# Squares of a recurrence taken on pairs, eight instead of four buffers for split weights, a later start of attention and a last output tile in halves, in one hybrid attention and recurrence layer

## The chip, the core and the metric

The kernel runs on one core of one Trainium2 chip, in one launch, in float32. The metric is the device time in microseconds (us) of a launch. The names of the engines are those of the profile: PE is the matrix engine, DVE the vector engine, ACT the scalar engine, POOL the general engine, SP the engine that issues most transfers.

## The reference

One layer on 512 tokens of width 2048. A normalized input is projected by `w_in` to queries, keys, values, two gates and the input of a gated linear recurrence. Eight heads of attention and a recurrence in both directions are each normalized, gated, and projected together by `w_out`.

```python
h = rms_norm(x, norm_w)
proj = h @ w_in                                  # (512, 2048) @ (2048, 4608)
q, k, v, g_attn, xr, g_lru = split(proj, SPLITS)
attn_out = attention_group(q, k, v, ...)         # RMS norm and rotation of q, k; softmax(q k) v; 8 heads
lru_out = lru_group(xr, ...)                     # h_fwd + h_bwd of two first-order recurrences over the tokens
mixed = concatenate([rms_norm(attn_out, attn_norm_w) * silu(g_attn),
                     rms_norm(lru_out, lru_norm_w) * silu(g_lru)])
return x + mixed @ w_out
```

Inside the recurrence: `a = exp(-8 r softplus(-lam))`, `h[t] = a[t] h[t-1] + sqrt(1 - a[t]^2) (i[t] xf[t])`, where `r` and `i` are sigmoids of two block-diagonal products.

## The kernel before

Every product is made of three matmuls: each operand is split into a high part (a rounding of the number, by a cast on ACT) and a low part (the rest, by a subtraction on DVE), and high x high, high x low and low x high are added up in PSUM (`mm3`, L142). For the weights this is `wsplit` (L195 to L201): a transfer brings 256 rows x 512 columns (`wr`, three buffers), and for each of the two halves of 128 rows (`k` is 0 or 1) ACT casts `wh` (L199) and DVE subtracts `wl` (L200). Tags `wh` and `wl` have four buffers each in the pool `xw`, two chunks' worth. A projection to 512 columns is eight such chunks; each chunk is four steps of six matmuls, and each step needs both halves of the chunk (`proj_feat`, `tok_block`).

The program runs in this order: the input is transposed, then the recurrence's input is projected (tag `pj`, PSUM banks), then the first half of the recurrence (`lru_half(0)`) beside the second half's projection, then the projection of keys and values (`kv_proj`) beside `lru_half(1)`, then the two projections of queries (`both`, that is `q_proj` twice) beside `kv`, which normalizes and rotates keys, then attention beside three gate projections (`gates`), then the last gate projection and the output projection (`outputs`). `weave` puts a stated number of projection steps between the pieces of a chain: where a chain yields 8, eight steps of six matmuls come next. The order of PE's instructions is therefore written out by hand. The order on ACT, DVE and POOL is made by a scheduler from priorities; each engine then works strictly in that order, and a wait holds everything behind it.

The recurrence goes by pairs of 128 channels (`lru_pair`, L374): products on PE, sigmoids on ACT (L407), then tanh (L417), exponentials (L423) and square roots (L427) on ACT, then on DVE L430, L431, four scans (L434) and two additions (L440) that write the pair's sum `hs`. L442 and L444 take the squares of `hs` on ACT, and L445 adds them up on POOL, for the norm.

Pools lie on two sides of SBUF, `left` and `right`. A pool opened where another was closed gets its memory, and each new tile there waits for the last use of the old tiles that lay in it (`reuse_waits="tile"`). After `kv_proj` the pool `lru`, with the recurrence's tiles `b4` and `k2`, is closed and `qkv` and `rot` are opened on the same side. `evac_tok` (L470, ACT) empties the PSUM banks of keys and values, so that the query projection can use them.

Of the kernel before, what the change touches and what calls it, by code (L numbers as in the profile page):

```python
# [55 lines left out]
def hybrid_kernel(  # L56
# [49 lines left out]
    def nm(s):  # L106
        cnt[0] += 1
        return f"{s}_{cnt[0]}"
# [77 lines left out]
    def wraw(w, r0, c0, nk=1):  # L186
# [3 lines left out]
        for k in range(nk):  # L190
            ks = slice(k * 2 // nk, (k + 1) * 2 // nk)
            nc.sync.dma_start(raw[:, ks, :], src[:, ks, :])
            yield raw

    def wsplit(raw, k):  # L195
# [3 lines left out]
        nc.scalar.copy(hi, raw[:, k, :])  # L199
        nc.vector.tensor_sub(lo, raw[:, k, :], f(hi))  # L200
        return hi, lo  # L201
# [172 lines left out]
    def lru_pair(n0, xrs, grs, steps, rest):  # L374

        xcs, cs, rs, is_, ths = [], [], [], [], []
        for n, xr, gr in zip((n0, n0 + 1), xrs, grs):
            with tc.high_priority(AHEAD // 2):
                gh, gl = k2(F32R, (P, 4, P)), k2(F32R, (P, 4, P))
                nc.scalar.copy(gh, gr)  # L380
                nc.vector.tensor_sub(gl, gr, f(gh))

                xc = k2()
                xcs.append(xc)
                nc.scalar.activation(
                    xc, xr, AF.Identity, bias=v1(R_CB + n), scale=v1(R_CW + 2 * NB + n)
                )
                for j, o in ((0, -2), (1, -1), (3, 1)):
                    d0, d1 = max(0, -o), SEQ - max(0, o)
                    nc.vector.scalar_tensor_tensor(  # L390
                        xc[:, d0:d1], xr[:, d0 + o : d1 + o], v1(R_CW + j * NB + n),
                        xc[:, d0:d1], op0=ALU.mult, op1=ALU.add,
                    )
                ch, cl = k2(F32R), k2(F32R)
                nc.scalar.copy(ch, xc)
                nc.vector.tensor_sub(cl, xc, f(ch))
                cs.append((gh, gl, ch, cl))
        for b, n in enumerate((n0, n0 + 1)):
            yield steps[b]
            gh, gl, ch, cl = cs[b]  # L400
            rs.append(b4())
            is_.append(b4())
            for dst, j0, bias in ((rs[b], 0, R_BA), (is_[b], 2, R_BX)):
                for d in range(2):
                    pg = mm()
                    mm3(pg, gh[:, j0 + d, :], gl[:, j0 + d, :], ch, cl, True, True)
                    nc.scalar.activation(  # L407
                        dst[:, d, :], pg, AF.Sigmoid, bias=v1(bias + d * NB + n)
                    )
            i = is_[b]  # L410
            nc.vector.tensor_mul(i, i, xcs[b][:, None, :].broadcast_to([P, 2, SEQ]))
        yield rest
        for b, n in enumerate((n0, n0 + 1)):
            ths.append(b4())
            for d in range(2):
                j = d * NB + n
                nc.scalar.activation(  # L417
                    ths[b][:, d, :], rs[b][:, d, :], AF.Tanh, scale=c2[:, j : j + 1]
                )
        for b, n in enumerate((n0, n0 + 1)):  # L420
            for d in range(2):
                j, r = d * NB + n, rs[b][:, d, :]
                last = nc.scalar.activation(r, r, AF.Exp, scale=c1[:, j : j + 1])  # L423

        with tc.issue_after(last.ins):
            for t in ths:
                nc.scalar.activation(t, t, AF.Sqrt, scale=-1.0)  # L427
        for b, n in enumerate((n0, n0 + 1)):
            a, i, t = rs[b], is_[b], ths[b]
            nc.vector.scalar_tensor_tensor(t, a, 1.0, t, op0=ALU.add, op1=ALU.mult)  # L430
            nc.vector.tensor_mul(i, i, t)  # L431
            for d in range(2):
                s = slice(None, None, -1 if d else 1)
                nc.vector.tensor_tensor_scan(  # L434
                    i[:, d, s], a[:, d, s], i[:, d, s], 0.0, ALU.mult, ALU.add
                )
# [3 lines left out]
            nc.vector.tensor_add(h, i[:, 0, :], i[:, 1, :])  # L440
            if n == 0:
                nc.scalar.activation(hsum, h, AF.Square)  # L442
            else:
                nc.scalar.activation(t[:, 0, :], h, AF.Square)  # L444
                nc.gpsimd.tensor_add(hsum, hsum, t[:, 0, :])  # L445


    def rope_consts():
# [172 lines left out]
    def group_rstd(src, name, n):  # L621

        pr = mm()
        for t in range(NT):
            nc.tensor.matmul(
                pr[:, t : t + 1], src[:, t * P : (t + 1) * P], ones[:, 0:1], start=True, stop=True
            )
# [50 lines left out]
    turn_of = [0]  # L678

    def wkept(n):  # L680
        i = turn_of[0] % 3
        turn_of[0] += 1
# [6 lines left out]
    def outputs(work):  # L689

        for c in range(DM // SEQ):
# [12 lines left out]
            def mult(k, s, ah, al, a, bh, bl, b_, last):  # L704
# [6 lines left out]
                for lh, rh in ((ah, bh), (ah, bl), (al, bh)):  # L711
# [3 lines left out]
                    )  # L715
                    fresh.discard(bank)

            def whole(t, ah, al, bh, bl, last):

                ts_ = slice(t % 2 * P, (t % 2 + 1) * P)  # L720
                for k in range(2):
                    a, w = 2 * k + t // 2, slice(2 * k, 2 * k + 2)
                    for j, (lh, rh) in enumerate(((ah, bh), (ah, bl), (al, bh))):
                        nc.tensor.matmul(  # L724
                            own[t], lh[:, a, ts_], rh[:, w].rearrange("p j e -> p (j e)"),
                            start=False, stop=last and k == 1 and j == 2, skip_group_check=True,
                        )

            for i, (r0, A) in enumerate(mixed):
                with tc.high_priority(AHEAD):  # L730
# [31 lines left out]
                        )  # L762
                        nc.vector.tensor_add(xt, xt, comb)
            with tc.high_priority(AHEAD):
                for t in (2, 3, 0, 1):
                    nc.vector.tensor_add(xt[:, t], own[t], xt[:, t])
                    nc.sync.dma_start(of[rows_[t], cs], xt[:, t])

# [42 lines left out]
                xstats()  # L811

    s1.close()
    sums["l"] = pools["rope"].tile([P, SEQ], F32, tag="hsum", name="hsum")
    lru_consts()
    fill = proj_feat(C_XR + SEQ, a2)
    weave(fill, lru_half(0, a1))
# [27 lines left out]
    weave(fill, kv(kvs))  # L845
    drain(fill)

    closed("rot", "rope")
    sums["a"] = pools["qkv"].tile([P, SEQ], F32, tag="asum", name="asum")
    opened("att", "right")  # L850
    for pair in hp:
        normed(pair)


    late = []

    def gates():
        todo = iter(())
        for n, (c0, row) in enumerate(((C_GL, R_LN), (C_GL + SEQ, R_LN + 4), (C_GA, R_AN))):
            acc, wait = [], 0  # L860
            for _ in proj_feat(c0, acc):
                if wait == 0:
                    wait = next(todo, 99)
                wait -= 1
# [7 lines left out]
    weave(fill, attention(rots))  # L872
    for _ in range(6):
        next(fill)
    r = group_rstd(sums["a"], "r_a", NH * HD)
    closed("att", "qkv")
    opened("fin", "right")
    for _ in range(3):
# [98 lines left out]
```

## Time and profile before

| | |
|---|---|
| three timed runs | 679.51, 677.59, 679.24 us; median 679.24 |
| the profiled execution | 677.44 us, with a span of 675.6 us from its first to its last instruction |
| busy, share of the span | PE 662.6 us (98%), DVE 481.6 (71%), ACT 335.5 (50%), POOL 72.4 (11%) |
| transfers | 71.06 MB, mean 105 GB/s |

A row of the profile's stretch by time has the start in us from the span's beginning, the duration, the engine, the line, the operation, its tiles and shapes, how many like it follow (x2), and in brackets the idle time before it and what ended that. "L" and a number is a line of the kernel before. The scheduled order of the program, shown in the next section, has no times in it; the numbers in its tile names tell one buffer from another.

### The profile page before, as it was taken

The page shows a single profiled execution, that of the slowest core. Times are in us where ns is not written, and L with a number is a line of the kernel's source. Part 1 is how long each engine was busy: PE and PEld are TensorE (multiplying, and loading weights), DVE is VectorE, ACT ScalarE, POOL GpSimd, SP SyncE. Part 2 cuts the span into 40 slices and gives each one's busy share as a digit, 9 for nine tenths or more (in the row PEclk, how much of TensorE's full clock was granted, in tenths as well). Part 3 has the DMA queues.
Part 4 walks back from the last instruction along what each step waited for, and adds up shares of the span by engine and source line. Part 5 has one row for each costly group of instructions (what it writes and reads, how often), then busy time and mean ns, then how long its engine had stood idle before and what let it go on. Part 6 is the DMA issues. An engine that isn't in the chain of part 4 may idle for free.

```text
span 675.6 us, 9495 instructions
## 1 busy us (share of the span) xinstructions
PE 662.6 (98%) x3590; PEld 568.6 (84%) x3590; DVE 481.6 (71%) x815; ACT 335.5 (50%) x585; POOL 72.4 (11%) x84
## 2 busy tenths in 40 slices
PE   9999999999899999899999999999999999999997
PEld 6888888887677888688888888888889999899996
DVE  4978697977486854755784558359869994976943
ACT  4534898588945426344664447345336333332320
POOL 0000001100122302111232222200000000000000
PEclk9999999999999999899999999999999999999999
DMA  8852252222223332222211222223335364363711
GB/s 282 281 144 78 74 151 67 90 63 72 84 66 121 94 94 90 66 63 63 61 38 58 63 64 62 64 63 94 112 106 159 124 199 131 114 215 92 241 41 62
DMA packets 43630, 71.06 MB, mean 105 GB/s; under 512 B 2761, under 2 KB 12865, under 8 KB 43585
## 3 DMA queue, kind: packets, MB, share of 16 engines
q1 hardware_dynamic: 43552, 70.45, 33.9%
q8 instruction: 28, 0.46, 0.3%
q14 instruction: 18, 0.14, 0.1%
q10 hardware_dynamic: 32, 0.01, 0.0%
HBM read 66.25 MB, written 4.19 MB: 104 GB/s over the span
## 4 chain that ended last, share of the span: by engine, by line
PE 82%; DVE 9%; ACT 5%; issue 2%; DMA 1%; POOL 0%; SPq 0%; ACTq 0%; DVEq 0%
PE pj L143 15%; PE pj L144 15%; PE pj L145 15%; PE pj L712 10%; PE mm L712 8%; PE mm L724 7%; PE mm L145 3%; PE mm L143 3%; PE mm L144 3%; PE mm L558 2%; DVE wl L200 2%; DVE b L434 2%; ACT wh L199 1%; DVE k L390 1%; DMA b<-in_x_dram 1%
## 5 line engine op out<-in xcount | busy, mean ns | idle before, releaser
L143 PE MATMUL pj<-x,wh 128*128 128x512 f32 x384 | 153.5, 400 | 0.0
L145 PE MATMUL pj<-x,wl 128*128 128x512 f32 x384 | 150.2, 391 | 0.0
L144 PE MATMUL pj<-x,wh 128*128 128x512 f32 x384 | 149.9, 390 | 0.0
L200 DVE TENSOR_TENSOR wl<-wr,wh 128x512 fp32r<-128x512 f32 x144 | 97.6, 698 | 55.3 <-ACT wh L199 53.4
L199 ACT CAST wh<-wr 128x512 fp32r<-128x512 f32 x144 | 86.4, 619 | 82.1 <-PE pj L145 34.9
L145 PEld LDWEIGHTS pj<-x,wl 128*128 128x128 f32 x384 | 72.2, 188 | 15.9 <-DVE wl L200 0.4
L144 PEld LDWEIGHTS pj<-x,wh 128*128 128x128 f32 x384 | 72.5, 189 | 14.1 <-issue 0.5
L143 PEld LDWEIGHTS pj<-x,wh 128*128 128x128 f32 x384 | 72.5, 189 | 14.0 <-issue 0.5
L143 PE MATMUL pj<-wh,x 128*128 128x512 f32 x192 | 75.8, 395 | 2.7 <-ACT kv L470 2.7
L144 PE MATMUL pj<-wl,x 128*128 128x512 f32 x192 | 75.0, 391 | 1.1 <-DVE wl L200 1.1
L145 PE MATMUL pj<-wh,x 128*128 128x512 f32 x192 | 74.9, 390 | 0.0
L712 PE MATMUL pj<-wh,ml 128*128 128x256 f32 x192 | 54.1, 282 | 0.0
L712 PE MATMUL pj<-wh,mh 128*128 128x256 f32 x192 | 54.0, 281 | 0.0
L712 PE MATMUL pj<-wl,mh 128*128 128x256 f32 x192 | 53.8, 280 | 0.0
L667 ACT CAST wh<-wr 128x768 fp32r<-128x768 f32 x24 | 20.1, 836 | 65.1 <-issue 46.6
L143 PEld LDWEIGHTS pj<-wh,x 128*128 128x128 f32 x192 | 36.0, 188 | 11.1 <-ACT kv L470 3.5
L144 PEld LDWEIGHTS pj<-wl,x 128*128 128x128 f32 x192 | 36.0, 188 | 9.8 <-DVE wl L200 2.1
L560 ACT CAST b<-mm 128x512 fp32r<-128x512 f32 x32 | 18.8, 587 | 48.3 <-PE mm L558 48.2
L145 PEld LDWEIGHTS pj<-wh,x 128*128 128x128 f32 x192 | 36.0, 188 | 7.5
L546 DVE TENSOR_REDUCE mx<-mm 128x1 f32<-128x512 f32 x32 | 22.0, 687 | 28.4 <-PE mm L145 28.4
L712 PE MATMUL mm<-wh,ml 128*128 128x256 f32 x144 | 40.5, 282 | 0.0
L712 PE MATMUL mm<-wh,mh 128*128 128x256 f32 x144 | 40.5, 281 | 0.0
(196 smaller groups left out, 1330.2 us busy)
## 6 DMA issues: line engine op xcount, KB each, us to landing
wr<-in_w_in_dram SPq DMA_DIRECT2D x71, 512.0 KB, 3.6
wr<-in_w_out_dram SPq DMA_DIRECT2D x32, 512.0 KB, 4.0
xt<-in_x_dram SPq DMA_DIRECT2D x16, 256.0 KB, 4.8
out_dram<-xt SPq DMA_DIRECT2D x16, 256.0 KB, 3.6
b<-in_x_dram SPq DMA_DIRECT2D x7, 512.0 KB, 8.6
k<-in_lru_wa_dram SPq DMA_DIRECT2D x8, 128.0 KB, 3.9
k<-in_lru_wx_dram SPq DMA_DIRECT2D x8, 128.0 KB, 3.1
b<-in_x_dram SPq DMA_DIRECT2D x2, 256.0 KB, 4.2
```

The source lines that it names most:

```text
L143: nc.tensor.matmul(acc, lh, rh, start=start, stop=False)
L144: nc.tensor.matmul(acc, lh, rl, start=False, stop=False)
L145: nc.tensor.matmul(acc, ll, rh, start=False, stop=stop)
L199: nc.scalar.copy(hi, raw[:, k, :])
L200: nc.vector.tensor_sub(lo, raw[:, k, :], f(hi))
L434: nc.vector.tensor_tensor_scan(i[:, d, s], a[:, d, s], i[:, d, s], 0.0, ALU.mult, ALU.add)
L546: nc.vector.tensor_reduce(mx, sc, axis=AX.X, op=ALU.max, negate=True)
L558: nc.tensor.transpose(pt[:, s * P : (s + 1) * P], p[:, s * P : (s + 1) * P], ident)
L560: nc.scalar.copy(pth[:, :, tt], p3)
L667: nc.scalar.copy(hi[:, to], part)
L712: nc.tensor.matmul(dst, lh[:, a, ts_], rh[:, b_, :], start=bank in fresh, stop=last and s == 1 and rh is bh and lh is al, skip_group_check ...
L724: nc.tensor.matmul(own[t], lh[:, a, ts_], rh[:, w].rearrange("p j e -> p (j e)"), start=False, stop=last and k == 1 and j == 2, skip_group ...
```

## The change

- The recurrence no longer squares each `hs` (L442 to L445 go). A new chain `lru_squares`, run inside `kv`, squares the four pairs at once (128x1024 on ACT) and adds them up on DVE; its sum has two rows of 512, and `group_rstd` takes a list and makes two small matmuls per token block instead of one. In `kv` the steps are dealt anew (24, 4, 4, 4 become 2, 2, 2, 20, 4, 4).
- `wsplit` takes its buffers from `xw` and a second pool, `wx`, in turn. `wx` exists from the closing of `lru` to the end of the query projections and lies on the right side, behind `qkv`; `rot` moves to the left side.
- `attention` yields 13 steps instead of 8 before its first product.
- The multiplication of the recurrence's pairs by their norm (`normed`, L635) stands in the text at steps 16, 20, 24 and 28 of the first gate projection instead of ahead of attention.
- In the last 512 columns of the output, the last 128 rows (`t == 1`) are computed as two halves of 256 columns, in two PSUM banks, each with its own addition and store.

```diff
 def wsplit(raw, k):
-    hi = pools["xw"].tile([P, SEQ], F32R, tag="wh", bufs=4, name=nm("wh"))
-    lo = pools["xw"].tile([P, SEQ], F32R, tag="wl", bufs=4, name=nm("wl"))
+    turn_of[0] += k
+    pool = pools["wx" if "wx" in pools and turn_of[0] % 2 else "xw"]
+    hi = pool.tile([P, SEQ], F32R, tag="wh", bufs=4, name=nm("wh"))
+    lo = pool.tile([P, SEQ], F32R, tag="wl", bufs=4, name=nm("wl"))
...
-            h, hsum = hp[n // 2][:, b, :], sums["l"]
-            nc.vector.tensor_add(h, i[:, 0, :], i[:, 1, :])
-            if n == 0:
-                nc.scalar.activation(hsum, h, AF.Square)
-            else:
-                nc.scalar.activation(t[:, 0, :], h, AF.Square)
-                nc.gpsimd.tensor_add(hsum, hsum, t[:, 0, :])
+            nc.vector.tensor_add(hp[n // 2][:, b, :], i[:, 0, :], i[:, 1, :])
+
+    def lru_squares():
+        hsum = pools["rot"].tile([P, 2, SEQ], F32, tag="hsum", name="hsum")
+        nc.scalar.activation(hsum, hp[0], AF.Square)
+        for pair in hp[1:]:
+            yield 2
+            sq = pools["rot"].tile([P, 2, SEQ], F32, tag="hsq", bufs=1, name=nm("hsq"))
+            nc.scalar.activation(sq, pair, AF.Square)
+            nc.vector.tensor_add(hsum, hsum, sq)
+        sums["l"] = [hsum[:, k, :] for k in range(2)]
...
+        yield from lru_squares()
         for h in range(NKV):
-            yield (24, 4)[h]
+            yield (20, 4)[h]
...
-        yield 4
         r = group_rstd(sums["l"], "r_l", NB * P)
...
     def attention(rots):
         qs, ps_, pts = {h: turned(rots[0], h) for h in range(2)}, {}, {}
-        yield 8
+        yield 13
...
     def group_rstd(src, name, n):
-            nc.tensor.matmul(
-                pr[:, t : t + 1], src[:, t * P : (t + 1) * P], ones[:, 0:1], start=True, stop=True
-            )
+            for k, part in enumerate(src):
+                nc.tensor.matmul(
+                    pr[:, t : t + 1], part[:, t * P : (t + 1) * P], ones[:, 0:1],
+                    start=k == 0, stop=k == len(src) - 1,
+                )
...
+                for half in range(2 if t == 1 and end else 1):
...
-                for t in (2, 3, 0, 1):
-                    nc.vector.tensor_add(xt[:, t], own[t], xt[:, t])
-                    nc.sync.dma_start(of[rows_[t], cs], xt[:, t])
+                parts = [(t, 0, SEQ, own[t]) for t in (2, 3, 0, 1)]
+                if end:
+                    parts[3:] = [(1, j * H, (j + 1) * H, lasts[j]) for j in range(2)]
...
     weave(kv_proj(), lru_half(1, a2))
     closed("lru")
+    opened("rot", "left")
     opened("qkv", "right")
-    opened("rot", "right")
+    opened("wx", "right")
...
-    for pair in hp:
-        normed(pair)
...
+                if n == 0 and k >= 16 and k % 4 == 0:
+                    normed(hp[k // 4 - 4])
```

Where this moves instructions is seen in the scheduled order. ACT, before, at the end of the key and value projection: `wh_1738` and `wh_1742` are the two halves of the query projection's first chunk, `b_...` are tiles of the recurrence's last two pairs, `kv_1638` and `kv_1640` the emptying of two PSUM banks.

```order
L199 CAST wh_1738<-wr_1736 128x512
L199 CAST wh_1742<-wr_1736 128x512
L407 ACTIVATE b_298_1581<-mm_1583,vec 128x512
L407 ACTIVATE b_298_1581<-mm_1588,vec 128x512
L407 ACTIVATE b_299_1582<-mm_1593,vec 128x512
L444 ACTIVATE b_264_1397<-hs_1413 128x512
L407 ACTIVATE b_299_1582<-mm_1598,vec 128x512
L417 ACTIVATE b_313_1646<-b_287_1518,c_93 128x512
L470 ACTIVATE kv_1638<-pj_1217,rstd 128x512
L444 ACTIVATE b_265_1400<-hs_1413 128x512
L417 ACTIVATE b_313_1646<-b_287_1518,c_93 128x512
L470 ACTIVATE kv_1640<-pj_1218,rstd 128x512
```

The same place of ACT after the change; `wh_1725` is the first half of the first chunk, `wh_1763` the second half of the second chunk.

```order
L203 CAST wh_1725<-wr_1723 128x512
L203 CAST wh_1763<-wr_1757 128x512
L411 ACTIVATE b_298_1569<-mm_1571,vec 128x512
L411 ACTIVATE b_298_1569<-mm_1576,vec 128x512
L411 ACTIVATE b_299_1570<-mm_1581,vec 128x512
L421 ACTIVATE b_313_1634<-b_287_1506,c_93 128x512
L411 ACTIVATE b_299_1570<-mm_1586,vec 128x512
L421 ACTIVATE b_313_1634<-b_287_1506,c_93 128x512
L479 ACTIVATE kv_1626<-pj_1209,rstd 128x512
L421 ACTIVATE b_314_1637<-b_298_1569,c_93 128x512
L479 ACTIVATE kv_1628<-pj_1210,rstd 128x512
```

And ACT after the change a little later, at the end of the recurrence's last pair (L431 is the square root, L427 of before); `wh_1729` is the second half of the first chunk, `wh_1759` the first half of the second, `wh_1797` the second half of the third.

```order
L427 ACTIVATE b_298_1569<-b_298_1569,c_92 128x512 x2
L431 ACT_TABLE_LOAD
L431 ACTIVATE b_313_1634<-b_313_1634 128x1024
L431 ACTIVATE b_314_1637<-b_314_1637 128x1024
L203 CAST wh_1729<-wr_1723 128x512
L203 CAST wh_1759<-wr_1757 128x512
L203 CAST wh_1797<-wr_1791 128x512
L491 ACTIVATE sh_1668,rr_1667<-kv_1626 128x128
```

The two L444 are gone from ACT, and the second half of the first chunk has moved from ahead of the last pair's tanh, exponentials and square roots to behind them. With its wait shown, `wh_1729` waits for a count of DVE that only DVE's last addition of the recurrence reaches.

DVE, before, at the end of the recurrence (L430, L431, L434 and L440 of the last pair; `wl_1887` and `wl_1891` are the query projection's fifth chunk):

```order
L431 TENSOR_TENSOR b_288_1519<-b_288_1519,b_313_1646 128x1024
L431 TENSOR_TENSOR b_299_1582<-b_299_1582,b_314_1649 128x1024
L434 SCALAR_TENSOR_TENSOR b_288_1519<-b_287_1518,b_288_1519 128x512 x2
L434 SCALAR_TENSOR_TENSOR b_299_1582<-b_298_1581,b_299_1582 128x512
L200 TENSOR_TENSOR wl_1887<-wr_1884,wh_1886 128x512
L200 TENSOR_TENSOR wl_1891<-wr_1884,wh_1890 128x512
L440 TENSOR_TENSOR hs_1662<-b_288_1519 128x512
L434 SCALAR_TENSOR_TENSOR b_299_1582<-b_298_1581,b_299_1582 128x512
L440 TENSOR_TENSOR hs_1662<-b_299_1582 128x512
```

DVE after the change (L435 is L431 of before, L438 is L434, L443 is L440):

```order
L435 TENSOR_TENSOR b_288_1507<-b_288_1507,b_313_1634 128x1024
L435 TENSOR_TENSOR b_299_1570<-b_299_1570,b_314_1637 128x1024
L438 SCALAR_TENSOR_TENSOR b_288_1507<-b_287_1506,b_288_1507 128x512 x2
L438 SCALAR_TENSOR_TENSOR b_299_1570<-b_298_1569,b_299_1570 128x512
L443 TENSOR_TENSOR hs_1650<-b_288_1507 128x512
L438 SCALAR_TENSOR_TENSOR b_299_1570<-b_298_1569,b_299_1570 128x512
L443 TENSOR_TENSOR hs_1650<-b_299_1570 128x512
L204 TENSOR_TENSOR wl_1730<-wr_1723,wh_1729 128x512
L204 TENSOR_TENSOR wl_1760<-wr_1757,wh_1759 128x512
L204 TENSOR_TENSOR wl_1798<-wr_1791,wh_1797 128x512
```

No weight subtraction stands inside the last pair any more, and the low part of the first chunk's second half, `wl_1730`, comes right behind the last addition.

More of the change, by code (lines that the diff above doesn't have):

```diff
@@ L716, in mult @@
                     fresh.discard(bank)
+            end = c == DM // SEQ - 1
+            lasts = [pj()[:, :H], own[1][:, H:]] if end else []
             def whole(t, ah, al, bh, bl, last):
                 ts_ = slice(t % 2 * P, (t % 2 + 1) * P)
[L721 to L727, printed above, removed]
+                for half in range(2 if t == 1 and end else 1):
+                    for k in range(2):
+                        a, w = 2 * k + t // 2, slice(2 * k, 2 * k + 2)
+                        dst = own[t].rearrange("p (j e) -> p j e", e=H)
+                        if t == 1 and end:
+                            dst, w = lasts[half], 2 * k + half
+                        for j, (lh, rh) in enumerate(((ah, bh), (ah, bl), (al, bh))):
+                            new = t == 1 and end and half == 0 and k == 0 and j == 0 and not last
+                            nc.tensor.matmul(
+                                dst, lh[:, a, ts_], rh[:, w], start=new,
+                                stop=last and k == 1 and j == 2, skip_group_check=True,
+                            )
             for i, (r0, A) in enumerate(mixed):
@@ L764, in outputs @@
             with tc.high_priority(AHEAD):
-                for t in (2, 3, 0, 1):
-                    nc.vector.tensor_add(xt[:, t], own[t], xt[:, t])
-                    nc.sync.dma_start(of[rows_[t], cs], xt[:, t])
+                parts = [(t, 0, SEQ, own[t]) for t in (2, 3, 0, 1)]
+                if end:
+                    parts[3:] = [(1, j * H, (j + 1) * H, lasts[j]) for j in range(2)]
+                for t, e0, e1, src in parts:
+                    nc.vector.tensor_add(xt[:, t, e0:e1], src, xt[:, t, e0:e1])
+                    nc.sync.dma_start(
+                        of[rows_[t], cs.start + e0 : cs.start + e1], xt[:, t, e0:e1]
+                    )
     ctx.enter_context(tc.manual_schedule(engines={mybir.EngineType.PE}))
@@ L813, in hybrid_kernel @@
     s1.close()
-    sums["l"] = pools["rope"].tile([P, SEQ], F32, tag="hsum", name="hsum")
     lru_consts()
@@ L860, in gates @@
             acc, wait = [], 0
-            for _ in proj_feat(c0, acc):
+            for k, _ in enumerate(proj_feat(c0, acc)):
+                if n == 0 and k >= 16 and k % 4 == 0:
+                    normed(hp[k // 4 - 4])
                 if wait == 0:
@@ L874, in hybrid_kernel @@
         next(fill)
-    r = group_rstd(sums["a"], "r_a", NH * HD)
+    r = group_rstd([sums["a"]], "r_a", NH * HD)
     closed("att", "qkv")
```

4 lines of the change are left out of this document (2 added, 2 removed).

## The prediction

> **What bounds the kernel now.** I read the page first, then PE's waits, then the stretches around each wait on PE, ACT and DVE.
>
> ```profile
> PE 662.6 (98%) x3590; PEld 568.6 (84%) x3590; DVE 481.6 (71%) x815; ACT 335.5 (50%) x585; POOL 72.4 (11%) x84
> PE pj L143 <- ACT kv L470: 2.7, 2, 1.7
> PE mm L143 <- ACT b L511: 1.9, 1, 1.9
> PE mm L145 <- DVE b L512: 1.2, 1, 1.2
> PE pj L144 <- DVE wl L200: 1.1, 2, 0.8
> ```
>
> PE is busy for 662.6 of 675.6 us, so PE bounds the kernel, and only its 13 us of idle time, the clock and the end can be gained, since the change takes no matmul away. Four waits carry more than half of the idle time (waits: total us, times, longest): PE waits at the start of the query projection for ACT to empty banks (2.7), at the start of attention for the split of the first queries (1.9 and 1.2), and in the query projection for weights' low parts (1.1).
>
> **The start of the query projection.** PE's stretch first:
>
> ```profile
> 169.97 0.50 PE L143 MATMUL pj<-wh,x 128*128 128x512 f32 x1 [1.03 <-ACT kv L470]
> 171.00 0.39 PE L144 MATMUL pj<-wl,x 128*128 128x512 f32 x1
> 171.23 0.39 PE L145 MATMUL pj<-wh,x 128*128 128x512 f32 x1
> 173.27 0.50 PE L143 MATMUL pj<-wh,x 128*128 128x512 f32 x1 [1.65 <-ACT kv L470]
> ```
>
> ACT's, from the same time and ahead of it:
>
> ```profile
> 141.01 0.62 ACT L395 CAST k<-k 128x512 fp32r<-128x512 f32 x1 [3.15 <-DVE k L390]
> 164.70 0.69 ACT L407 ACTIVATE b<-mm,vec 128x512 f32<-128x512 f32 x1 [0.32 <-DVE b L434]
> 167.52 0.63 ACT L444 ACTIVATE b<-hs 128x512 f32<-128x512 f32 x1 [2.13 <-DVE hs L440]
> 171.40 0.63 ACT L444 ACTIVATE b<-hs 128x512 f32<-128x512 f32 x1 [1.49 <-DVE hs L440]
> 172.55 0.67 ACT L470 ACTIVATE kv<-pj,rstd 128x512 f32<-128x512 f32 x1
> 177.95 1.95 ACT L423 ACTIVATE b<-b,c 128x512 f32<-128x512 f32 x3
> 179.81 1.13 ACT L199 CAST wh<-wr 128x512 fp32r<-128x512 f32 x2
> 181.56 1.28 ACT L427 ACT_TABLE_LOAD   x1
> 182.85 2.01 ACT L427 ACTIVATE b<-b 128x1024 f32<-128x1024 f32 x2
> ```
>
> and DVE's:
>
> ```profile
> 183.95 2.36 DVE L430 SCALAR_TENSOR_TENSOR b<-b,b 128x1024 f32<-128x1024 f32 x2 [2.21 <-ACT b L427]
> 186.23 1.28 DVE L200 TENSOR_TENSOR wl<-wr,wh 128x512 fp32r<-128x512 f32 x2
> 193.07 1.26 DVE L200 TENSOR_TENSOR wl<-wr,wh 128x512 fp32r<-128x512 f32 x2
> 194.25 0.68 DVE L440 TENSOR_TENSOR hs<-b 128x512 f32<-128x512 f32 x1
> 196.10 1.59 DVE L440 TENSOR_TENSOR hs<-b 128x512 f32<-128x512 f32 x1
> ```
>
> ACT's two squares waited 2.13 and 1.49 us for DVE, and the emptying of the banks (L470) stood behind them: that is why PE waited here. The recurrence's last pair ran on until DVE's addition ended at 196.10 + 1.59 = 197.69, while PE was already in the query projection.
>
> **The change, part by part, in us.**
>
> *Squares and buffers at the start of the query projection.* Taking the squares away removes ACT's two waits, and so PE's two. But in the new order of ACT the cast of the first chunk's second half, `wh_1729`, stands behind the last pair's square roots and waits for DVE's last addition, and its low part `wl_1730` follows that addition on DVE. Every step of the projection needs both halves, and PE's order is fixed; so PE does the three matmuls of the first half and then stands until the recurrence has ended. The doubled buffers lie in the memory of the recurrence, and this one in a tile that is used to the very end. Before, PE did four to five chunks in this time (24 matmuls at 0.23, from 171.00 to 171.23, are 5.5 a chunk). When the wait ends is worked out so:
>
> ACT, from the start of the sigmoid at 164.70 to the square roots at 182.85, took 18.15. In the new order the same way holds ten activations of 128x512, four emptyings, one weight cast and two table loads. Three activations take 1.86 to the next start (177.95 to 179.81), 0.62 each, though recorded at 0.65; an emptying, recorded at 0.67, then 0.6; a cast 0.55 (half of 1.13); a table load 1.29 (181.56 to 182.85). 10 x 0.62 + 4 x 0.6 + 0.55 + 2 x 1.29 = 11.7. The sigmoid's own wait of 0.32 is for a tile that the squares held back, and goes as well. The square roots then start at 164.38 + 11.7 = 176.1, and DVE's L430 1.10 later as before, at 177.2. DVE took 197.69 - 183.95 = 13.74 from there to its last addition; two pairs of weight subtractions (2 x 1.2) leave it, and the last addition takes 0.68 instead of 1.59, as the one at 194.25 did. That makes 13.74 - 2.4 - 0.9 = 10.4, and the end comes at 187.6. A cast (0.6) and a subtraction (0.7) later PE has `wl_1730`: 188.9.
>
> Part of this may come sooner, because POOL's additions go too:
>
> ```profile
> 125.63 3.34 POOL L445 TENSOR_TENSOR hsum<-hsum,b 128x512 f32<-128x512 f32 x1 [17.93 <-ACT b L444]
> 135.10 1.55 POOL L445 TENSOR_TENSOR hsum<-hsum,b 128x512 f32<-128x512 f32 x1 [6.13 <-ACT b L444]
> 168.29 1.39 POOL L445 TENSOR_TENSOR hsum<-hsum,b 128x512 f32<-128x512 f32 x1 [31.64 <-ACT b L444]
> 168.54 2.23 DVE L411 TENSOR_TENSOR b<-b,k 128x1024 f32<-128x1024 f32 x1
> 171.29 1.21 DVE L411 TENSOR_TENSOR b<-b,k 128x1024 f32<-128x1024 f32 x1
> ```
>
> Under such an addition a DVE instruction took 2.23, without it 1.21: 1.0 more. Two of them ran between 125 and 137, ahead of the point at 141.01 where ACT waited 3.15 for DVE. So ACT may run up to 2 ahead from there on. Nothing says how much of that reaches the end; between 186.9 and 188.9 I take 187.0, since that wait at 141.01 is what ACT's later rows follow from. PE's matmul with `wl_1730`, at 171.00 before, comes at 187.0: +16.0. The old wait of the second step is gone (173.27 less 171.23 less a matmul of 0.23, and 0.1 because the matmul after a wait takes 0.50 instead of 0.39): -1.9. Together +14.1.
>
> *The clock after that wait.* No row shows PE idle for 18 us. The nearest:
>
> ```profile
> 275.20 0.39 PE L145 MATMUL pj<-x,wl 128*128 128x512 f32 x1
> 277.46 0.51 PE L143 MATMUL mm<-kt,b 128*128 128x512 f32 x1 [1.87 <-ACT b L511]
> 279.38 0.80 PE L145 MATMUL mm<-kt,b 128*128 128x512 f32 x1 [1.17 <-DVE b L512]
> 275.00:280.00 5.00, 1.96 (x7) 0.91 (x6) 4.85 (x9) 2.04 (x4) 0.00 (x0) 0.88 0.34 104
> 280.00:285.00 5.00, 5.00 (x21) 4.20 (x20) 1.55 (x3) 2.65 (x4) 0.70 (x1) 0.78 0.30 101
> 170.00:175.00 5.00, 3.35 (x14) 2.44 (x14) 2.56 (x4) 3.60 (x7) 1.46 (x1) 1.00 0.00 2
> ```
>
> After idle times of 1.87 and 1.17 the granted clock fell to 0.88 and 0.78 in two stretches of 5: 0.6 + 1.1 = 1.7 of PE's time. After 1.65 within 170 to 175 it stayed at 1.00. So the price lies between 0 and twice 1.7; I take 1.7, as the idle time is surely no shorter than that of the dip. Sum so far +15.8.
>
> The Trainium skill ("TensorE: Matmul & The Clock Gate", Part 1: The HAM clock gate) says that PE falls to half rate after an idle window of about 3.4 us and is released only after a busy window, and that the windows run free of the program. By that rule the wait surely costs one such window and up to two at half rate, an estimate of 1.7 to 3.4 us, and the sum below would be up to 1.7 higher; the dip in this trace agrees with one window, and no run here yet shows a long wait.
>
> *Low parts that were late (L200).* Two waits of 1.1 in all, and 0.1 after each, go: in the new order DVE does the keys' rotation while the projection is still in its first chunks, with the buffers of three chunks loaded. -1.3, and 0 if DVE is late again.
>
> *Attention 13 steps in.* Five more steps of six matmuls at 0.23 are 6.9 of cover. The split of the first queries was 1.87 and then 1.17 late, in all some 3.1 and the clock's 1.7: all of it fits under 6.9. -4.8; at least -3.1. The same five steps are missing behind attention, where DVE is the one to be late:
>
> ```profile
> 475.00:500.00 25.00, 25.00 (x112) 20.67 (x111) 19.13 (x29) 9.44 (x15) 0.00 (x0) 1.00 0.33 105
> 510.00:525.00 15.00, 15.00 (x129) 15.00 (x128) 14.95 (x21) 9.18 (x11) 0.00 (x0) 1.00 0.61 194
> ```
>
> DVE was idle for 5.9 in the first stretch and for nothing in the second, where the output's operands are made. 6.9 less room against 5.9 of slack there: between 0 and 2; I take 0.5, since DVE's order puts the weights first.
>
> *The rest.* Four more small matmuls for the norm, and the last tile:
>
> ```profile
> 240.03 0.95 PE L625 MATMUL mm<-ones,hsum 128*128 128x1 f32 x8
> 240.84 0.49 PE L143 MATMUL pj<-wh,x 128*128 128x512 f32 x1
> 671.50 0.69 DVE L766 TENSOR_TENSOR xt<-mm,xt 128x512 f32<-128x512 f32 x1 [0.67 <-PE mm L724]
> 427.94 0.42 DVE L573 COPY av<-mm 128x256 f32<-128x256 f32 x1
> ```
>
> The eight records of four matmuls took 0.81 less one ordinary 0.23: +0.6. The last addition falls from 0.69 to about 0.42, and the last store has half the bytes: -0.3 to -1.0, I take -0.4. The squares on pairs (four of about 1.0, as half of L427's 2.01) and their sums on DVE (three of about 1.2, as L411's 1.21) I cost at nothing: sixteen chunks of query projection, 88 of PE's time, lie over them. Without that cover they would cost at most their 7.6. The norm's multiplication stays ahead of attention in DVE's order, so its new place in the text is worth nothing.
>
> **Sum**: 15.8 - 1.3 - 4.8 + 0.5 + 0.6 - 0.4 = +10.4. Against the profiled execution's 677.44 that is 687.8; the median of the three runs stands 1.8 above that execution, and the same on top of it would be 689.6. I forecast between them, 688.7: slower by 1.4%.
>
> **Rivals.**
>
> *Faster: the new buffer is free early.* If the tile's memory were released before PE comes the start would lose its waits (2.7, and 0.2 after them), and the sum be -2.9 - 1.3 - 4.8 + 0.5 + 0.6 - 0.4 = -8.3: 670. It decides if `wh_1729` is there by 169. Against it stand ACT's and DVE's strict orders, in which it comes behind square roots that cannot start before their exponentials. 0.04.
>
> *The recurrence's end comes much sooner.* If, freed of weight work, it ended near 182 instead of 185.7 (187.0 less cast and subtraction), the sum would be about +6.5: 684 or 685; with the clock's price gone as well, 683. At 175 the change would break even. DVE's 10.4 of scans and sums in a row speak against it, since each waits for the one before. 0.08.
>
> *A second wait, at the output.* If the 6.9 of room that attention takes from DVE's work behind it came back in full as PE waiting for the output's operands, 6.4 more than I charged, the time would be 695. For it speaks DVE's full stretch from 510 to 525, against it the 5.9 of idle time before; it begins to cost once DVE is later than it was by what PE's matmuls now leave it. With part of it, and with the clock low for twice as long, 693 and up: 0.13.
>
> **Numbers.** My forecast holds 0.75, with 684 to 693 as its own range. With most of the second and third rivals, 8 in 10 reach from 682.5 to 695. A measurement here tells 0.3% (2 us) from no change: slower 0.94 (mine, the third rival and most of the second), the same 0.02 (the rest of the second), faster 0.04.
>
> **What would show it.** Right: PE idle for 16 to 19 us from about 169, ended by L204 or L203 with `wl` or `wh`; ACT's wait there put down to DVE `hs`; a clock well below 1 in the slice behind it; no wait of L470, nor of the first queries at attention; POOL without its seven additions. Wrong: no idle time there, or one under 10 us. The forecast fails in size if the clock stays low for longer, or if PE waits for weights between 500 and 540.

## The result, and the profile after

Four executions after the change took 688.93 to 689.73 us, median 689.11; four of before on the same chip took 677.59 to 679.51, median 678.62. The ratio is 1.0157 with a 95% interval of 1.0138 to 1.0175: the change makes the kernel slower by 1.6%. The profiled execution after the change took 688.93 us, with a span of 687.1.

The first part of the page, then the longest of PE's waits (line, what it waited for: total us, times, longest):

```profile
PE 663.7 (97%) x3610; PEld 571.0 (83%) x3610; DVE 486.8 (71%) x819; ACT 332.0 (48%) x581; POOL 57.2 (8%) x77
PE pj L143 <- ACT wh L203: 17.2, 1, 17.2
```

PE is busy for about as long as before (663.7 against 662.6 us), and the span is 11.5 longer. Of the four waits that carried PE's idle time before none is left; one of 17.2 us stands in their place. (The two waits left lie in the first 7 us. The one for the input is 1.5 instead of 0.5, but at 150 us PE is where it was: 150.04 against 150.02.) POOL's seven additions are gone. The wait in PE's stretch by time:

```profile
168.53 0.39 PE L145 MATMUL pj<-wh,x 128*128 128x512 f32 x1
186.11 0.79 PE L143 MATMUL pj<-wh,x 128*128 128x512 f32 x1 [17.20 <-ACT wh L203]
186.84 0.79 PE L144 MATMUL pj<-wl,x 128*128 128x512 f32 x1
187.43 0.63 PE L145 MATMUL pj<-wh,x 128*128 128x512 f32 x1
187.86 0.63 PE L143 MATMUL pj<-wh,x 128*128 128x512 f32 x1
191.27 0.51 PE L145 MATMUL pj<-wh,x 128*128 128x512 f32 x1
191.62 0.40 PE L143 MATMUL pj<-wh,x 128*128 128x512 f32 x1
```

ACT and DVE in the same time:

```profile
173.88 2.00 ACT L431 ACTIVATE b<-b 128x1024 f32<-128x1024 f32 x2
185.44 1.66 ACT L203 CAST wh<-wr 128x512 fp32r<-128x512 f32 x3 [9.56 <-DVE hs L443]
```
```profile
174.97 2.36 DVE L434 SCALAR_TENSOR_TENSOR b<-b,b 128x1024 f32<-128x1024 f32 x2 [3.52 <-ACT b L431]
184.72 0.69 DVE L443 TENSOR_TENSOR hs<-b 128x512 f32<-128x512 f32 x1
186.09 1.89 DVE L204 TENSOR_TENSOR wl<-wr,wh 128x512 fp32r<-128x512 f32 x3 [0.68 <-ACT wh L203]
```

The cast at 185.44 is `wh_1729`. ACT stood for 9.56 us ahead of it, because the cast waits for DVE's last addition of the recurrence (184.72 + 0.69 = 185.41). PE's wait ends when the cast does. The stretches show what became of the clock (columns: PE, PEld, DVE, ACT, POOL busy, the granted clock, DMA share, GB/s):

```profile
165.00:170.00 5.00, 3.92 (x18) 2.91 (x16) 3.05 (x4) 4.97 (x8) 0.00 (x0) 1.00 0.00 0
170.00:175.00 5.00, 0.00 (x0) 0.00 (x0) 0.72 (x2) 4.97 (x8) 0.00 (x0) 0.60 0.00 0
175.00:180.00 5.00, 0.00 (x0) 0.00 (x0) 5.00 (x5) 0.88 (x1) 0.00 (x0) 0.50 0.00 0
180.00:185.00 5.00, 0.00 (x0) 0.00 (x0) 4.97 (x6) 0.00 (x0) 0.00 (x0) 0.50 0.00 0
185.00:190.00 5.00, 3.89 (x9) 2.77 (x10) 3.45 (x8) 4.56 (x18) 1.60 (x4) 0.50 0.37 112
190.00:195.00 5.00, 5.00 (x20) 4.06 (x19) 4.13 (x13) 4.77 (x11) 2.98 (x3) 0.85 0.62 210
```

The clock falls to half about 2 us into the wait (0.60 as the mean of 170 to 175), stays there throughout, and comes back only 5.4 us after PE has resumed, at 191.5. Until then a matmul comes every 0.43 us instead of every 0.23.

At attention and at the end, the rows that answer to those of before:

```profile
298.87 0.39 PE L145 MATMUL pj<-x,wl 128*128 128x512 f32 x1
299.10 0.39 PE L143 MATMUL mm<-kt,b 128*128 128x512 f32 x1
683.19 0.28 PE L742 MATMUL mm<-wh,ml 128*128 128x256 f32 x1
252.88 1.84 PE L635 MATMUL mm<-ones,hsum 128*128 128x1 f32 x16
254.58 0.48 PE L143 MATMUL pj<-wh,x 128*128 128x512 f32 x1
```
```profile
295.00:300.00 5.00, 5.00 (x24) 4.11 (x23) 2.86 (x6) 1.24 (x2) 0.00 (x0) 1.00 0.36 105
487.00:512.00 25.00, 25.00 (x112) 20.71 (x111) 23.53 (x34) 10.17 (x16) 0.00 (x0) 1.00 0.42 124
522.00:537.00 15.00, 15.00 (x129) 15.00 (x128) 14.95 (x22) 9.11 (x11) 0.00 (x0) 1.00 0.61 193
```
```profile
683.51 0.42 DVE L787 TENSOR_TENSOR xt<-mm,xt 128x256 f32<-128x256 f32 x1 [0.29 <-PE mm L742]
```

Attention's first product follows without a wait and at full clock. The output's first matmul stands at 519.62 instead of 507.69, so the stretches 475 to 500 and 510 to 525 of before are 487 to 512 and 522 to 537 here. DVE has 1.5 us of slack left in the first, where it had 5.9, and is as full as before in the second (14.95); PE has no wait there. The small matmuls of the norm take 1.70 instead of 0.81, and the last addition 0.42 instead of 0.69.

### The profile page after: what moved, and what is told of

Read it like the earlier page. It is cut to its first block, busy times and chain, and to the rows that moved or that the text cites. A ratio compares the mean times of both kernels' runs of the same rounds, so it can differ in the third digit from the quotient of the medians.

```text
span 687.1 us, 9526 instructions
## 1 busy us (share of the span) xinstructions
PE 663.7 (97%) x3610; PEld 571.0 (83%) x3610; DVE 486.8 (71%) x819; ACT 332.0 (48%) x581; POOL 57.2 (8%) x77
## 4 chain that ended last, share of the span: by engine, by line
PE 95%; ACT 2%; DVE 2%; DMA 1%; issue 0%; SPq 0%; ACTq 0%
PE pj L143 19%; PE pj L144 19%; PE pj L145 19%; PE pj L721 10%; PE mm L721 7%; PE mm L742 6%; PE mm L145 3%; PE mm L143 3%; PE mm L144 3%; PE mm L567 2%; PE mm L229 1%; DMA b<-in_x_dram 1%; DVE b L438 1%; PE mm L516 1%; PE mm L266 0%; ACT b L427 0%
## 5 line engine op out<-in xcount | busy, mean ns | idle before, releaser
L204 DVE TENSOR_TENSOR wl<-wr,wh 128x512 fp32r<-128x512 f32 x144 | 100.8, 717 | 53.2 <-ACT wh L203 53.1
L143 PE MATMUL pj<-wh,x 128*128 128x512 f32 x192 | 77.2, 402 | 17.2 <-ACT wh L203 17.2
L144 PE MATMUL pj<-wl,x 128*128 128x512 f32 x192 | 76.4, 398 | 0.0
L145 PE MATMUL pj<-wh,x 128*128 128x512 f32 x192 | 76.0, 396 | 0.0
```

The lines of the kernel that those rows point to most:

```text
L143: nc.tensor.matmul(acc, lh, rh, start=start, stop=False)
L144: nc.tensor.matmul(acc, lh, rl, start=False, stop=False)
L145: nc.tensor.matmul(acc, ll, rh, start=False, stop=stop)
```

## The experiments

My theory: the whole loss is the one cast that waits for memory of the recurrence, together with the clock that this wait costs; everything else in the change is a gain or free. The rival: the scheduler's new order or the squares' new place costs the time, and the buffers are incidental. Ratios are to before, on the same chip, with 95% intervals.

### e1: the change without the second pool

```diff
-    opened("wx", "right")
```

> The changed kernel with all weights in the pool of before (wx is never opened); squares on pairs, attention 13 steps in, the moved multiplication and the halves stay. Theory A, the whole loss is the cast that waits for memory of the recurrence: no idle time of PE at the start of the query projection, the emptying waits gone with the squares (-2.9), attention -4.8, +0.5 behind it, +0.6 for the norm, -0.4 at the end, late low parts between 0 and -1.3: 669 to 671 us for a profiled execution, 1.0% to 1.3% faster than before. Theory B, the loss comes from the new order that the squares' removal gives, whatever the buffers: PE still stands 10 us or more and the time stays above 680 us.

Measured: 667.14 us (666.83 to 667.24), ratio 0.9834 [0.9819, 0.9848]; span 665.4, granted clock 1.000. PE's only waits are two at the program's start:

```profile
PE mm L801 <- POOL ones L151: 1.1, 1, 1.1
PE mm L229 <- DMA b<-in_x_dram: 0.4, 1, 0.4
```

Theory A holds, and the time is 1.9 below the range that I had written (669 to 671). More than half of this comes ahead of the gate projections, whose first matmul stands at 259.54 instead of 264.44: 4.9 sooner, where my terms gave 2.3 to 3.6. A wait of 0.4 at 161, which I had not counted, goes too, and the late low parts had cost 1.6. One line less makes the change 22 us faster, and this version beats both kernels. The low parts, late twice before, are not late here, with four buffers as before: four buffers are enough for them in the new order.

### e2: before with the second pool alone

```diff
+    turn_of = [0]
 def wsplit(raw, k):
+    turn_of[0] += k
+    pool = pools["wx" if "wx" in pools and turn_of[0] % 2 else "xw"]
...
+    opened("rot", "left")
     opened("qkv", "right")
-    opened("rot", "right")
+    opened("wx", "right")
```

> Before with the second pool alone (rot moved to the left to make room); squares, attention and output as before. Theory A: the same cast now stands behind the last two squares as well. Square roots at 182.85 - 0.6 (one cast less ahead) = 182.2, last addition 1.1 + 11.3 later at 194.6 at most, then square, cast and subtraction 1.9: PE resumes at 193 to 197 where it went on at 171.0, so +22 to +26, less 1.9 and 1.3 for waits that go, plus 2 to 3 for the clock: 698 to 703 us, a longer wait than in the changed kernel. Theory B: no long wait, 676 to 679 us.

Measured: 701.15 us (700.16 to 702.14), ratio 1.0336 [1.0317, 1.0355]. The longest of PE's waits, and ACT's stretch:

```profile
PE pj L143 <- ACT wh L203: 23.3, 1, 23.3
```
```profile
191.33 0.63 ACT L448 ACTIVATE b<-hs 128x512 f32<-128x512 f32 x1 [4.37 <-DVE hs L444]
193.38 0.63 ACT L448 ACTIVATE b<-hs 128x512 f32<-128x512 f32 x1 [1.42 <-DVE hs L444]
193.92 1.12 ACT L203 CAST wh<-wr 128x512 fp32r<-128x512 f32 x2
```

The buffers alone cost more than the whole change. The cast stands behind the last two squares here. In the changed kernel, which has neither these squares nor POOL's additions, the wait ends 8.5 us sooner (186.11 against 194.57). Of the waits that I had expected to go, one of 1.1 for a bank and one of 0.8 for a low part stay. Theory B falls.

### e8: the second pool from the third chunk on

```diff
-    pool = pools["wx" if "wx" in pools and turn_of[0] % 2 else "xw"]
+    pool = pools["wx" if "wx" in pools and turn_of[0] >= 26 and turn_of[0] % 2 else "xw"]
```

(24 chunks come ahead of the query projection, so 26 is its third chunk.)

> The changed kernel with the second pool used from the third chunk's second half on. Theory A (the wait ends with the recurrence, wherever it begins): PE does two chunks more (10.9 us), stands from about 179 to 188 for 8 to 10 us, ended by the cast or the subtraction of that half; against e1 +8.8, +2 to 3 for the clock, +1.3 for the pace: 678 to 682 us, ratio 1.000 to 1.005. Theory B (a fixed price of taking the new pool): 17 us of idle time as in the changed kernel, 687 us or more.

Measured: 679.92 us (679.36 to 681.51), ratio 1.0028 [1.0016, 1.0039]. The longest of PE's waits, and PE's row behind it:

```profile
PE pj L143 <- ACT wh L203: 8.7, 1, 8.7
```
```profile
188.66 0.79 PE L143 MATMUL pj<-wh,x 128*128 128x512 f32 x1 [8.66 <-ACT wh L203]
```

PE did two chunks more and stood for 8.7 instead of 17.2, until 188.66; DVE's last addition began at 187.26. The wait has no fixed price: it lasts from the first use of the new memory to the end of the recurrence.

### e3: the second pool from the fifth chunk on

The same line with 28 instead of 26.

> The changed kernel, but the first four chunks of the query projection take their buffers from the old pool and the second pool is used from the fifth chunk's second half on. PE reaches that chunk at 167 + 22 = 189 us, about when the recurrence ends (185 to 188). Theory A: no long wait, 668 to 671 us; against e1 the doubled buffers are worth 0 to 1.3 us (late low parts). Theory B (doubled buffers wait wherever they begin, or bring nothing): a wait of more than 2 us at that chunk, 672 us or more.

Measured: 668.93 us (668.67 to 669.59), ratio 0.9862 [0.9846, 0.9879]. ACT's cast into the new pool still waits for the recurrence, but PE isn't there yet:

```profile
189.86 1.67 ACT L203 CAST wh<-wr 128x512 fp32r<-128x512 f32 x3 [4.36 <-DVE hs L443]
```

No wait of PE is left in the query projection, as expected. But it is 1.8 us slower than e1, where I had expected it 0 to 1.3 faster. 0.3 of this is there when the query projection begins (PE is 0.43 later already 7 us into the program, behind the input's first transfer), 0.35 comes with the fifth chunk's first matmuls. The rest grows evenly through the query projection: from 0.65 at 191 us to 1.87 at its end (260 us), at a granted clock of 1.00. Counted over chunks with nothing else between their 24 matmuls, a matmul comes every 0.2313 us instead of every 0.2267 (the expectation below has 0.2314 and 0.2272, a coarser count). e9 asks why.

### e9, e11, e10: why the pace falls with the second pool

e9 uses the second pool alone from the fifth chunk on (`turn_of[0] - k >= 28` as the condition), so nothing alternates.

> The changed kernel with the old pool alone for four chunks and the second pool alone from the fifth chunk of the query projection to its end, so four buffers at any time and no alternation. With the doubled buffers from the fifth chunk (e3) the matmuls of the query projection came every 0.2314 us, with the old pool alone (e1) every 0.2272 at the same granted clock, 1.3 us over 300 matmuls. Theory A (place in memory): 0.2314 again, about 1.3 us slower than e1. Theory B (the alternation between two pools): 0.2272, and 667 to 668 us if no wait at the fifth chunk is over 0.5.

Measured: 669.17 us (668.62 to 669.37), ratio 0.9863 [0.9845, 0.988]; a matmul of the query projection comes every 0.2333 us, counted the same way. Neither theory has the number, but B falls and A's cause stands: without alternation the pace is slower still, so the buffers' place makes it, and e3's 0.2313 lies between the two places. The old pool lies at multiples of 64 bytes, the new one at odd multiples of 32, so I tried that:

```diff
+    opened("pad", "right").tile([P, 8], F32, tag="pad", name="pad")
     opened("wx", "right")
```

> e9 (second pool alone from the fifth chunk) with an empty tile of 32 bytes per partition ahead of the second pool, which puts its buffers at multiples of 64 bytes (145344 instead of 145376; the old pool's lie at multiples of 64 already). Theory A (an odd multiple of 32 bytes as start of the streamed operand costs the pace): 0.2272 us per matmul of the query projection instead of e9's 0.2336, 667 to 667.9 us, that is 1.3 to 2 us below e9. Theory B (the place of the pool itself, far or near, not its last bits): 0.2336 as in e9 and 669.2 us.

> e1 (no second pool) with the same 32 empty bytes at the head of the whole right side, so that all tiles there (keys, values, softmax weights, heads, gates, the output's split operands) start at multiples of 64 bytes instead of odd multiples of 32. Theory A: the streamed operands of attention and of the output, about 205 us of PE's time, run 0.5% to 2.8% faster: 1 to 5 us below e1, 662 to 666 us. Theory B: 667 us as e1, within 0.7.

Measured: e11 668.92 us (668.7 to 669.55), ratio 0.9875 [0.9859, 0.989], with 0.2333 us a matmul; e10 667.68 (667.34 to 668.04), ratio 0.9855 [0.9837, 0.9873], with 0.2267. Both times theory B: a multiple of 64 bytes instead of an odd multiple of 32 does nothing. PE's matmuls in the same 35 us, of e1, e9 and e11 (first number in brackets):

```profile
195.00:230.00 35.00, 35.00 (x158) 28.95 (x157) 26.21 (x47) 19.00 (x53) 6.52 (x8) 1.00 0.35 103
```
```profile
195.00:230.00 35.00, 35.00 (x154) 28.09 (x153) 26.83 (x54) 19.88 (x58) 8.38 (x12) 1.00 0.31 90
```
```profile
195.00:230.00 35.00, 35.00 (x154) 28.08 (x153) 26.82 (x52) 19.86 (x58) 8.04 (x11) 1.00 0.32 93
```

The second pool lies some 58 KB further up in each partition. Whether distance, neighbours or something else counts stays open.

### e7: the wait filled with matmuls

```diff
                     mm3(acc[t], lh[kk][:, ts_], ll[kk][:, ts_], wh, wl, kk == 0, kk == nk - 1)
+                    if c0 == C_Q and w is w_in and c == t == k == 0:
+                        for _ in range(76):
+                            nc.tensor.matmul(acc[1], lh[0][:, ts_], wh, start=True, stop=True,
+                                             skip_group_check=True)
```

> The changed kernel with 76 more matmuls of 128x512 in the long wait, behind the third matmul of the query projection, into a bank that a later start overwrites: they use 76 x 0.22 = 16 to 17 of the 17.3 us in which PE stands, so PE stays busy up to the wait's end and nothing else is moved. Theory A (the clock): half-speed matmuls from 186 to 191.6 go; the dozen excess gaps there, 2.8 us in all, go, 685.9 to 687.0 us, ratio 1.011 to 1.0125, and the granted clock is 1.00 throughout. Theory B (the slow matmuls behind the wait are held by weights, or by memory): the time stays at 689, ratio 1.0157.

Measured: 686.98 us (686.93 to 687.2), ratio 1.0127 [1.011, 1.0145]: 2.1 below the changed kernel. The stretches:

```profile
180.00:185.00 5.00, 5.00 (x23) 4.13 (x23) 4.97 (x6) 0.00 (x0) 0.00 (x0) 1.00 0.00 0
185.00:190.00 5.00, 4.77 (x20) 3.37 (x19) 3.45 (x7) 4.37 (x18) 1.40 (x4) 1.00 0.37 96
```

76 matmuls whose result is overwritten make the kernel faster: PE stays at full clock and has begun 14 of the projection's own matmuls by 190, where the changed kernel has begun 9 (the 20 of the row count the last of the 76 too). The wait itself ends at the same time (the first matmul with `wl` at 187.03 against 186.84). The two medians were taken beside different runs of before (medians 678.16 and 678.62), so the 2.1 holds to about 1. Behind the wait a few low parts, squares and rotations of the keys stand in a slightly different order on ACT and DVE; PE waits for none of them. The trace gives the same: the eleven matmul starts behind that one took 4.78 us in the changed kernel and 2.66 here, 2.1 less.

### e5 and e6: attention and squares by themselves

e5 is before with `yield 13` instead of `yield 8`.

> Before with 13 instead of 8 steps ahead of attention and nothing else. Prediction's term: -4.8 (at least -3.1: waits of 1.87 and 1.17; the clock dip of 1.7 goes with them), +0.5 (0 to 2) behind attention: 672.6 to 675 us for a profiled execution, no wait for the first queries, clock 1.00 from 275 to 285. Rival: the five steps that are missing behind attention come back as a wait of PE for weights between 500 and 540, and the time stays within 0.3% of before.

Measured: 672.88 us (672.59 to 673.1), ratio 0.9919 [0.9904, 0.9934]; the span is 670.8, 4.8 below that of before. The first queries' wait is gone, the clock is 1.00, and the wait behind attention that the rival foresaw does not appear, though DVE has less room ahead of the output (23.55 of 25 us busy from 470 to 495, where before has 19.13 in the same part of the program, from 475 to 500):

```profile
275.00:280.00 5.00, 5.00 (x23) 4.14 (x23) 4.93 (x9) 2.13 (x4) 0.00 (x0) 1.00 0.34 105
280.00:285.00 5.00, 5.00 (x25) 4.14 (x25) 2.77 (x5) 2.58 (x4) 0.00 (x0) 1.00 0.60 173
470.00:495.00 25.00, 25.00 (x112) 20.71 (x111) 23.55 (x34) 10.39 (x16) 0.00 (x0) 1.00 0.40 124
```

e6 is before with `lru_squares`, the two-row norm and `rot` on the left, and the old buffers and attention.

> Before with the squares on pairs alone (rot on the left, steps dealt anew, two-row sum for the norm); buffers, attention and output as before. Theory A (squares of the last pairs held the emptying of the banks, squares on pairs are hidden): the two waits of 1.03 and 1.65 at the start and 0.2 behind them go, the wait of 0.4 at 161 too, late low parts 0 to -1.3, norm +0.6: -2.4 to -4.0, 673.4 to 675.0 us for a profiled execution (ratio 0.994 to 0.9965); attention's first waits stay. Theory B (the squares as pairs delay the keys' rotation or weights): a new wait in the query projection, ratio 0.998 or above.

Measured: 673.89 us (672.38 to 674.55), ratio 0.9928 [0.991, 0.9946]; span 672.5. The waits at the start of the query projection and the late low parts are gone, those of the first queries stay:

```profile
PE mm L143 <- ACT b L516: 1.9, 1, 1.9
PE mm L145 <- DVE b L517: 1.2, 1, 1.2
```
```profile
270.00:275.00 5.00, 1.94 (x8) 1.00 (x6) 4.93 (x10) 2.32 (x4) 0.00 (x0) 0.89 0.38 105
275.00:280.00 5.00, 5.00 (x14) 4.06 (x15) 1.95 (x4) 2.65 (x4) 0.48 (x1) 0.50 0.34 108
280.00:285.00 5.00, 5.00 (x22) 4.04 (x21) 1.32 (x3) 1.84 (x4) 0.92 (x2) 0.93 0.00 0
```

PE reaches attention 4.5 earlier than before (272.95 against 277.46), but leaves it only 3.1 earlier: behind the same two waits the clock stays low for twice as long (5 x (0.11 + 0.50 + 0.07) = 3.4 us lost, against 1.7 before). The traces' clock stands at half from 273.9 to 280.7 here and from 278.8 to 282.2 in before, twice as long. The gain of the squares is thus larger than the ratio shows: at the same mean granted clock of 0.997, executions of e6 took 672.4 and 672.9 us, those of before on the same chip 677.4 to 678.2. The price of those waits is not fixed. Since attention 13 steps in takes both waits away, e1 doesn't pay it.

## Why the prediction was right, step by step

The time (689.11 against the forecast 688.7) came out by the mechanism foreseen, and e2, e8 and e1 show that mechanism: more wait with the cast later, less with its first use later, none without the pool. That the two numbers lie so close is in part luck, as the item on the buffers below shows. By steps, from the two traces:

| step | predicted | measured |
|---|---|---|
| matmul with `wl_1730`, 171.00 before | 187.0 (+16.0) | 186.84 (+15.8) |
| old waits for the banks | -1.9 | -1.9, no such wait left |
| the clock behind the wait | +1.7 (0 to 3.4) | +2.1 (e7) |
| pace of the query projection | not foreseen | +1.7 (369 matmuls x 0.0046) |
| late low parts | -1.3 | -1.6, no such wait left |
| small matmuls of the norm | +0.6 | +0.9 |
| attention 13 steps in | -4.8 | -5.0; alone -4.8 (e5's span) |
| five steps less behind attention | +0.5 (0 to 2) | +0.2 |
| last tile in halves | -0.4 | -0.6 |
| sum | +10.4 | +11.6; spans +11.5 |

How the rows come about: in before the two late low parts and the matmuls behind them began 1.14, 0.34, 0.73 and 0.34 after the one ahead, against an ordinary 0.23, so 1.6. The 369 matmuls are those of the query projection from 191.62 on, where the clock is full again. From the first matmul of the gate projections to the last of attention PE took 170.53 before and 172.40 after, with five steps (6.83) more in it, so -4.96. From there to the first matmul of the output it took 72.72 before and 65.92 + 6.83 = 72.75 after, and from there to the last matmul 163.38 and 163.57: +0.2 together. From the start of the last matmul to the span's end it was 4.5 and is 3.9.

- *The end of the recurrence* was worked out in two pieces, and both came as forecast. ACT took 11.8 from the sigmoid at 162.12 to the square roots at 173.88 (forecast 11.7), and DVE 185.41 - 174.97 = 10.4 from L430 to the end of the last addition (forecast 10.4). What came sooner was the start: the sigmoid stood at 162.12, not at 164.38. These 2.3 are what I had allowed for POOL's vanished additions (up to 2), and of that allowance I took nearly all. ACT's cast that waited at 141.01 before ran at 137.59 after; of these 3.4 some 1.2 went again on the way to the sigmoid, half of it in a wait for PE (0.60 ahead of two weight casts at 159.37). In the trace of before two DVE instructions under POOL's additions ahead of that point took 1.0 longer each (L390 1.78 at 127.74 instead of 0.74, L200 1.70 at 135.50 instead of 0.68), which is 2 of the 3.4. No run took POOL's additions alone away, so that it was POOL which freed DVE there remains argued.
- *The clock* was foreseen too low by 0.4, inside its bounds. The Trainium skill ("TensorE: Matmul & The Clock Gate", Part 1: The HAM clock gate) gives half rate after an idle window of about 3.4 us and until a busy window has passed. The granted clock of 0.50 agrees with this, and the 2.1 lies in the prediction's estimate of 1.7 to 3.4. The start does not agree: the clock fell when PE had stood for 2.1 us (168.9 to 171.0), and in before and e6 behind waits of 1.9 and 1.2 us.
- *Squares and their sums at nothing*: PE waits for them neither in e1 nor in e6. Right.
- *Doubled buffers* had no cost of their own in the sum except the wait. That is the term left out: 1.7 for the pace, which no row of before could show, since no weights lay there. It put the sum 1.1 below the profiled execution (687.8 against 688.93). The forecast of 688.7 made up for it by luck: the 0.9 that it adds to the sum is half of the 1.8 between the median of before and its profiled execution. Executions of before differ so among themselves (see the last section). The four of the changed kernel do not: all lie within 0.8 us at a mean granted clock of 0.985, so the addition stands for nothing in them; without it the forecast is the sum, 687.8.
- *The rivals*: a free buffer would have given 670, and e3, where PE comes late enough, gave 668.93. The recurrence did not end much sooner (185.41, where the sum had 185.7). The second wait at the output did not come: DVE used 4.4 of the 5.9 of slack that it had ahead of the output and was never late.

The change thus holds some 11 us of gain (e1) and 22 of loss from one line. The doubled buffers gain nothing that e1 doesn't have.

## What to carry to other kernels

A new pool in memory that a chain has just used begins when that chain ends, not when the pool is opened: look for the last reader of the very tile that the first buffer falls on, and for what waits behind that buffer in each engine's fixed order. If it is the chain's last instruction, leave the first few uses in the old memory, or do without. Waits of PE of 8.7, 17.2 and 23.3 us (e8, the changed kernel, e2) each cost some 2 us more behind them, at half clock. Where such a wait can't be removed, matmuls whose result nobody uses can win that back, as they did in e7.

## What the runs showed of the hardware

- The same weights streamed from another place in memory gave 0.2333 us a matmul instead of 0.2267 (2.9%) at a granted clock of 1.00 (e1, e9). Starting at a multiple of 64 bytes instead of an odd multiple of 32 changed nothing (e11: 0.2333). The cause stays open.
- The price of a short wait isn't fixed: waits of 1.9 and 1.2 us cost 1.7 us of clock in before and 3.4 in e6, with nothing changed at that place but the time at which they come. Nor is it fixed for one kernel: of 30 executions of before, run beside the experiments, 3 took 676.4 us at a mean granted clock of 0.999, 16 took 677.4 to 678.4 at 0.997, and 11 took 678.5 to 680.4 at 0.995. The four of e5, without these two waits, lie within 0.5 us. A half-clock stretch of 3.4 us in 676 lowers the mean by 0.0025, so none, one and two of them would fit; only the profiled execution's trace, with one, was kept.
- The stretches at half clock last 3.4 us (before), 6.8 (e6), 10.2 (e8), 20.5 (the changed kernel) and 27.3 (e2): 1, 2, 3, 6 and 8 times 3.4. They began 2.1, 2.2 and 3.5 us after PE had stopped in the changed kernel, e2 and e8.
- 76 matmuls whose result nobody uses, in a wait of 17.2 us, kept the granted clock at 1.00 and saved 2.1 us (e7).
